# DeltaNet mixer: evacuation steps metered between filler matmuls and pinned on VectorE, decay rows queued behind the inverse, heads split one at a time

## The chip, the cores and the metric

The kernel runs on one core of one Trainium2 chip. The time is the device time of one execution in microseconds, and the number that counts is the median over several runs. The core has a matrix engine (TensorE, PE in the profile), a vector engine (VectorE, DVE), an activation engine (ScalarE, ACT), GpSimd (POOL) and SyncE (SP), which issues nearly all the transfers (DMA). Each engine takes its instructions in a fixed order that is settled when the program is compiled, and waits on semaphores for what other engines make. PSUM holds matmul results in eight banks; SBUF holds everything else.

## What is computed

The reference is a decoder trunk of two layers over 1024 positions of width 1024: layer 0 mixes with a gated DeltaNet, layer 1 with sliding-window attention, and each layer goes on with a convolutional MLP and a per-layer embedding. The change lies in the DeltaNet mixer, and for a small part in the output projection that both mixers share. Cut to what matters:

```python
proj = x @ w_in
qkv = silu(causal_dwconv(proj[..., :3 * hk], conv_w))        # 4 taps along the positions
z = proj[..., 3 * hk:4 * hk]                                 # the gate, 8 heads of 128
q, k = l2norm(q), l2norm(k)
g = -exp(a_log) * softplus(a_in + dt_bias)                   # decay, per head and position
# per head, in chunks:
gcs = cumsum(g); decay = exp(gcs_i - gcs_j) for i >= j
lmat = strictly lower part of (beta * k k^T * decay)
u0, wk = (I + lmat)^-1 [beta * v, beta * exp(gcs) * k]
for each chunk:
    u = u0 - wk s;  o = (q * exp(gcs)) s + (q k^T * decay) u
    s = exp(gcs_last) * s + k_dec^T u
o = rmsnorm(o, norm_w) * silu(z)
out = o @ w_out
```

## The kernel before

Activations are held transposed: 128 channels on the partitions, 1024 positions along the free dimension. A tile of that shape is called a slot tile; 40 slots of SBUF are handed out by a small list (`Slots.get` takes the slot that has been free longest, `put` gives one back). A tile that takes over a slot waits for the last reader of the tile that had it.

*Projections as filler.* Each of the 32 tiles of q, k, v and gate (`act_tile`, `gate_tile`, L452 to L482) is a product of eight 128x128 weight blocks with the normalized input, in three passes each (high and low parts in float32r, `passes`, L215), for two halves of 512 positions: 24 matmuls a half. These products are written as a Python generator, `stream` (L496), that yields after each matmul. The rest of the mixer calls `fill(n)` (L484) wherever TensorE would wait for another engine, and so n filler matmuls are written out there. `until` (L513) fills until a tile that is needed exists. When the projections are used up, the generator goes on with the first part of the output projection (`OutProj.first`, L865), five of the eight heads' share.

*What follows a half tile.* As soon as its 24 matmuls are written, the generator writes the evacuation (L468: PSUM times the norm's row factor, on VectorE, into a padded tile `zp`), the convolution (`conv`, L320: a first tap on ScalarE, three taps as scalar_tensor_tensor on VectorE, L323) and a SiLU on ScalarE (L470). The gate has only an evacuation (L480) and a SiLU.

*Orders.* In the mixer TensorE's instructions are pinned: `E.pinned` (L327) calls `keep_in_program_order`, named `pin`, which puts an instruction behind the one written before it on the same engine. The other engines are pinned in a few places only; elsewhere the compiler's scheduler chooses an order from its own idea of when inputs are ready.

*One head* (loop at L823). `stage1(h)` (L594) loads two rows of decays from DRAM, spread over all partitions (512 KB each, L599 and L606), makes the decay matrix E from the first (L601 on VectorE, L603 and L604 on ScalarE), transposes k, sums its squares on ScalarE (L616), makes kd (L618) and the triangular matrix A (L637), sends A through DRAM to GpSimd, which inverts its 16x16 diagonal blocks in 30 small steps (L652 to L658), and stores them to DRAM (L660, L661). `stage1c(h)` does the same for q and makes the masked products (L682). `stage2(h-1)` (L765) is the recurrence of the head before: eight chunks, each with the chain product, t (L779), product, u (L782 on ScalarE), product, state update st (L792 for the first chunk, L794 after), with 5, 5 and 4 fillers between. `norm_factor` and `stage2b(h-1)` (L810) scale the output of a head (L812), transpose it and multiply it by the gate (L819). `stage1v(h)` turns v. `stage1b(h)` (L708) loads the inverted blocks as R and X (L713, L714) and completes the inverse from blocks of 16 to 128 by products on TensorE (L721 to L761). For head 0, 100 fillers stand ahead of `stage1b`.

*Start.* Four half tiles (k and q of head 0) are begun while the input comes in: they hold all three PSUM banks of the fillers' pool `mm` and one of the three of the pool `d`. Behind them VectorE and ScalarE work out the decays for all heads (L519 to L570), 84 fillers, and then the cumulated decays are written to DRAM (L589).

*Output projection.* `split_first` (L862) splits five heads' outputs at once into high and low parts (`split`, L245: ScalarE copies the high part, VectorE subtracts, L251), 1024 positions wide; then `first(m)` runs eight tiles of 30 matmuls as filler. The attention layer uses the same class, and its stream waits until five outputs exist (L1163).

Of the kernel before, what the change touches and what calls it, by code (L numbers as in the profile page):

```python
# [8 lines left out]
F32 = mybir.dt.float32  # L9
# [7 lines left out]
P = 128  # L17
# [3 lines left out]
NCH = T // P  # L21
# [26 lines left out]
SLOTW = T + 4  # L48
SKEW = 8
NLAST = 4  # L50

# [45 lines left out]
def hs(h):  # L97
    return slice(h * 512, (h + 1) * 512)
# [11 lines left out]
def kernel(  # L110
# [215 lines left out]
    def delta_layer():  # L326
# [123 lines left out]
        outs = []  # L450

        def act_tile(m, name, res, key):  # L452

            begun = m % HA == 0 and m // HA <= 1
            if not begun:
                wh, wl = load_w(a_in[m], D)
            for i in range(2):
# [5 lines left out]
                if i == 0:  # L463
                    z = S.wide("zp")
                    G.memset(z[:, 0:CA - 1], 0.0)
                    y = S.get(name)
                a, b = i * 512, (i + 1) * 512
                V.tensor_tensor(z[:, CA - 1 + a:CA - 1 + b], ps, rb[:, a:b], MUL)  # L468
                conv(y, z, aconv[:, m * CA:(m + 1) * CA], CA, a, b)
                A.activation(y[:, a:b], y[:, a:b], AF.Silu)  # L470
            res[key] = y

        def gate_tile(h, res):
            wh, wl = load_w(a_in[24 + h], D)
            for i in range(2):
                ps = pmt()
                yield from passes(ps, wh, wl, xs, i)
                if i == 0:
                    z = S.get("zs")
                V.tensor_tensor(z[:, hs(i)], ps, rb[:, hs(i)], MUL)  # L480
            A.activation(z[:, :], z[:, :], AF.Silu)
            res[h] = z  # L482

        def fill(n=1 << 30):  # L484

            for _ in range(n):
                if next(main, S) is S:
                    break

        def load_h(t, m):  # L490
            nc.sync.dma_start(t[:, 0:T], xT[m * P:(m + 1) * P, :])

        op = OutProj(a_out, outs, load_h)
        q, k, v, zs, st = {}, {}, {}, {}, {}

        def stream():  # L496
            yield from act_tile(HA, "kT", k, 0)
            yield from act_tile(0, "qT", q, 0)
            yield from act_tile(2 * HA, "vT", v, 0)
            yield from gate_tile(0, zs)  # L500
            for h in range(1, HA):
                yield from act_tile(HA + h, "kT", k, h)
                yield from act_tile(h, "qT", q, h)
                yield from act_tile(2 * HA + h, "vT", v, h)
                yield from gate_tile(h, zs)
            for xh, xl in xs:
# [85 lines left out]
        fill(FG3)  # L592

        def stage1(h, kT):  # L594
            hsl = slice(h * NCH, (h + 1) * NCH)
            junk = sm.tile([P, P], F32, tag="junk", name="junk", bufs=1)
            ssk = sm.tile([P, NCH], F32, tag="ssk", name="ssk")
            rw = S.get("row")
            nc.sync.dma_start(rw[:, :], rowd[0, h:h + 1, :].partition_broadcast(P))  # L599
            ee = S.get("E")  # L600
# [4 lines left out]
            rw = S.get("row")  # L605
            nc.sync.dma_start(rw[:, :], rowd[1, h:h + 1, :].partition_broadcast(P))  # L606

# [100 lines left out]
        def stage1b(h, s):  # L708
# [3 lines left out]
            r = S.get("R")  # L712
            nc.sync.dma_start(r.c3(), mat(xd[par, 1]))  # L713
            nc.sync.dma_start(x.c3(), mat(xd[par, 0]))  # L714
# [50 lines left out]
        def stage2(h, s, FS=FS, FO=FO):  # L765
# [5 lines left out]
            for c in range(NCH):  # L771
# [3 lines left out]
                else:  # L775
                    E.matmul(ch(ps, 0), ch(kT, c), st, start=True, stop=True)
                    fill(FS)
                    t = sm.tile([P, P], F32, tag="t", name="t")
                    V.scalar_tensor_tensor(t, ch(ps, 0), s["nse"][:, c:c + 1], ch(vv, c), MUL, ADD)  # L779
                E.matmul(ch(ps, 1), ch(r, c), t, start=True, stop=True)  # L780
# [8 lines left out]
                if c < NCH - 1:  # L789
                    st2 = sm.tile([P, P], F32, tag="st", name="st")  # L790
                    if c == 0:
                        V.tensor_copy(st2, ch(ps, 2))  # L792
                    else:
                        V.scalar_tensor_tensor(  # L794
                            st2, st, egl[:, h * NCH + c:h * NCH + c + 1], ch(ps, 2), MUL, ADD)
                    st = st2
# [13 lines left out]
        def stage2b(h, s, zs, n=FV):  # L810
            o, kd, f = s["vv"], s["kd"], s["f"]
            pin(V.tensor_tensor(o.c3(), o.c3(), col(f[:, :], NCH, P), MUL))  # L812
            fill(n)
# [33 lines left out]
    class OutProj:  # L847
# [13 lines left out]

        def split_first(self):  # L862
            self.xs = self.parts(0, NP1)

        def first(self, m):  # L865
            t = S.get("h")
            self.load_h(t, m)
            self.h.append(t)
            wh, wl = load_w(self.w[m, :, 0:NP1 * P], NP1 * P)
            for h in range(2):  # L870
                ps = pmt()
                yield from passes(ps, wh, wl, self.xs, h)
                V.tensor_tensor(t[:, hs(h)], t[:, hs(h)], ps, ADD)
            if m == KT - 1:
# [98 lines left out]
    def swa_layer(xs, nrm, hd):  # L973
# [181 lines left out]
        def stream():  # L1155
# [6 lines left out]
            S.put(rb)  # L1162
            while len(outs) < NP1:  # L1163
                yield
            op.split_first()
            for m in range(KT):
# [545 lines left out]
```

## Time and profile before

| | us |
|---|---|
| median of 3 runs | 2745.27 (2741.79 to 2749.13) |
| the profiled execution | 2740.68 |
| its span, first to last instruction | 2738.8 |
| TensorE busy | 2640.8 (96%) |
| VectorE busy | 1792.9 (65%) |
| ScalarE busy | 1114.9 (41%) |
| GpSimd busy | 1191.4 (43%) |
| mean granted TensorE clock | 0.99 |

The profile is that of one execution. A row of instructions names the line of the kernel, the engine, the operation, the tile written and the tiles read (buffer numbers left out), and in brackets how long the engine was idle before it and what ended that idle time. A row of waits reads "engine, tile, line, then what it waited for: us in total, times, longest". A row of a stretch of time gives the busy time of TensorE, its weight loads, VectorE, ScalarE and GpSimd with the counts of instructions, then the granted TensorE clock (1.00 is full speed), the DMA engines' busy share and GB/s. Of a matmul only the start is exact; ends are modelled.

### The profile page before, as it was taken

To read this page: it belongs to the slowest core of one execution; us is meant where nothing else is said; L and a number is where in the kernel's file an instruction comes from. 1 tells how busy PE (TensorE), PEld (TensorE's weight loads), DVE (VectorE), ACT (ScalarE), POOL (GpSimd) and SP (SyncE) were. 2 spreads that over 40 slices of the span, in tenths; PEclk is the share of its full clock that TensorE was granted. 3 is DMA by queue.
4 is the path that set the end of the run, shared out by engine and by line. 5 is a ranking of instruction groups with operands and counts; after the bars stand their busy time and mean duration, and the time that the engine had idled before them with its cause. 6 is when DMAs were issued, how large, how long until landed. Compare 5 with 4: busy or idle time off the path is not lost. (4 is left out here: it accounts for less than half of the span.)

```text
span 2738.8 us, 35465 instructions
## 1 busy us (share of the span) xinstructions
PE 2640.8 (96%) x12914; PEld 2130.2 (78%) x12914; DVE 1792.9 (65%) x2645; ACT 1114.9 (41%) x2176; POOL 1191.4 (43%) x1132
## 2 busy tenths in 40 slices
PE   9899999999999999999999999999999999999998
PEld 7788787878777887888778776667778888888786
DVE  6555555564787777677774437775877767677745
ACT  5443443442643333333353225554533333333443
POOL 4444443442554444444532323335644444444354
PEclk9999999999999999999999999999999999999999
DMA  5222211232325555555432221122255555554323
GB/s 176 89 73 58 67 55 56 67 95 78 109 84 187 181 182 180 203 198 181 161 117 71 90 59 49 46 92 100 81 187 187 182 191 178 199 198 167 103 93 110
DMA packets 167215, 340.85 MB, mean 124 GB/s; under 512 B 38912, under 2 KB 91648, under 8 KB 167040
## 3 DMA queue, kind: packets, MB, share of 16 engines
q1 hardware_dynamic: 166176, 337.20, 37.2%
q8 instruction: 102, 1.67, 0.3%
q10 hardware_dynamic: 864, 1.38, 0.1%
q14 instruction: 73, 0.60, 0.1%
HBM read 232.56 MB, written 99.68 MB: 121 GB/s over the span
## 5 line engine op out<-in xcount | busy, mean ns | idle before, releaser
L202 POOL TENSOR_TENSOR wlo<-wraw,whi 128x512 fp32r<-128x512 f32 (+1 forms) x204 | 269.8, 1340 | 380.6 <-ACT whi L199 344.1
L153 PE MATMUL mm<-xh,whi 128*128 128x512 f32 x856 | 356.2, 416 | 3.9 <-ACT xh L255 2.8
L153 PE MATMUL mm<-xh,wlo 128*128 128x512 f32 x856 | 347.9, 406 | 0.0
L153 PE MATMUL mm<-xl,whi 128*128 128x512 f32 x856 | 346.0, 404 | 0.8 <-DVE xl L256 0.8
L212 POOL TENSOR_TENSOR dlo<-draw,dhi 128x256 fp32r<-128x256 f32 (+1 forms) x160 | 163.1, 1020 | 332.9 <-ACT dhi L211 295.7
L1234 POOL TENSOR_TENSOR wlo<-wraw,whi 128x512 fp32r<-128x512 f32 x132 | 192.6, 1466 | 147.7 <-ACT whi L1233 145.4
L1234 POOL TENSOR_TENSOR wlo<-sa,whi 128x512 fp32r<-128x512 f32 x132 | 194.1, 1470 | 141.0 <-ACT whi L1233 141.0
L153 PE MATMUL d<-gh,dhi 128*128 128x512 f32 x576 | 228.7, 397 | 4.7 <-DVE h L1350 4.2
L153 PE MATMUL d<-gl,dhi 128*128 128x512 f32 x576 | 226.9, 394 | 0.7 <-DVE gl L251 0.7
L153 PE MATMUL d<-gh,dlo 128*128 128x512 f32 x576 | 227.3, 395 | 0.0
L1350 DVE TENSOR_TENSOR h<-h,d 128x512 f32<-128x512 f32 x288 | 193.1, 680 | 32.6 <-PE d L153 32.2
L199 ACT CAST whi<-wraw 128x1024 fp32r<-128x1024 f32 (+3 forms) x122 | 100.1, 822 | 238.5 <-PE mm L153 123.4
L153 PEld LDWEIGHTS mm<-xh,wlo 128*128 128x128 f32 x856 | 163.3, 191 | 33.6 <-POOL wlo L202 0.2
L153 PEld LDWEIGHTS mm<-xh,whi 128*128 128x128 f32 x856 | 163.6, 191 | 30.6 <-ACT xh L255 3.2
L153 PEld LDWEIGHTS mm<-xl,whi 128*128 128x128 f32 x856 | 163.5, 191 | 26.9 <-DVE xl L256 1.4
L153 PE MATMUL mm<-t34h,whi 128*128 128x512 f32 x352 | 139.4, 396 | 3.7 <-DVE zv L1394 3.0
L153 PE MATMUL mm<-t34l,whi 128*128 128x512 f32 x352 | 139.6, 397 | 3.2 <-POOL t34l L919 3.2
L153 PE MATMUL mm<-x1l,whi 128*128 128x512 f32 x352 | 138.9, 395 | 0.2 <-DVE x1l L919 0.2
L153 PE MATMUL mm<-x1h,whi 128*128 128x512 f32 x352 | 138.8, 394 | 0.0
L153 PE MATMUL mm<-t34h,wlo 128*128 128x512 f32 x352 | 138.7, 394 | 0.0
L323 DVE SCALAR_TENSOR_TENSOR yf<-zv,fcv,yf 128x1024 f32<-128x1024 f32 (+1 forms) x92 | 121.5, 1321 | 26.3 <-ACT yf L321 26.2
L153 PE MATMUL mm<-x1h,wlo 128*128 128x512 f32 x352 | 138.2, 392 | 0.0
(382 smaller groups left out, 6564.0 us busy)
## 6 DMA issues: line engine op xcount, KB each, us to landing
hf<-h SPq DMA_DIRECT2D x160, 512.0 KB, 3.3
h<-hf SPq DMA_DIRECT2D x160, 512.0 KB, 4.2
wraw<-f_up SPq DMA_DIRECT2D x88, 512.0 KB, 3.3
draw<-f_down SPq DMA_DIRECT2D x144, 128.0 KB, 2.1
wraw<-a_in SPq DMA_DIRECT2D x32, 512.0 KB, 3.5
wraw<-g_w SPq DMA_DIRECT2D x24, 512.0 KB, 3.3
row<-rowd SPq DMA_DIRECT2D x16, 512.0 KB, 3.7
wraw<-b_in SPq DMA_DIRECT2D x12, 512.0 KB, 3.6
```

Source lines behind the costliest of these rows:

```text
L153: i = nc.tensor.matmul(*a, **k)
L199: A.copy(hi, raw)
L202: G.tensor_tensor(lo[:, i:j], raw[:, i:j], hi[:, i:j].bitcast(F32), SUB)
L212: G.tensor_tensor(lo, raw, hi[:, :].bitcast(F32), SUB)
L323: V.scalar_tensor_tensor(dst[:, a:b], z[:, a + i:b + i], w[:, i:i + 1], dst[:, a:b], MUL, ADD)
L1234: G.tensor_tensor(lo, src, hi.bitcast(F32), SUB)
L1350: V.tensor_tensor(t[:, hs(h)], t[:, hs(h)], ps, ADD)
```

## The change

Three things are edited, all in how and where instructions are written out; no matmul is added or removed.

First, what follows a half tile is no longer written at once. The evacuation and each of the three taps become steps in a list, `later`. `fill` takes one step from the list after every third filler (`EACH = 3`); `until` takes steps before it fills; `flush` empties the list ahead of the output projection. Each step's VectorE instruction is pinned, and so are t, the state updates and the low parts of the first output split.

Second, the loads of the decay rows (`load_row`) are put on SyncE's queue behind the load of R written last (`r_load`), which is that of the head before, and behind each other. The first head's rows have none ahead.

Third, the output projection's first tile (m = 0) splits one head at a time, in halves, and runs that head's six matmuls before it goes to the next head; both PSUM banks are taken together. It waits for each head's output alone, so that the attention layer's own wait for five is gone. Beside it the scaling of a head's output (L812) is done in two halves.

```diff
+EACH = 3
...
+        later = []
         def act_tile(m, name, res, key):
...
+            def evacuate(i, ps):
+                if i == 0:
+                    t.extend((S.wide("zp"), S.get(name)))
+                    G.memset(t[0][:, 0:CA - 1], 0.0)
+                z, y = t
+                a, b = i * 512, (i + 1) * 512
+                pin(V.tensor_tensor(z[:, CA - 1 + a:CA - 1 + b], ps, rb[:, a:b], MUL))
+                A.activation(y[:, a:b], z[:, a:b], AF.Copy, scale=w[:, 0:1])
+
+            def tap(i, j):
+                z, y = t
+                a, b = i * 512, (i + 1) * 512
+                pin(V.scalar_tensor_tensor(y[:, a:b], z[:, a + j:b + j], w[:, j:j + 1], y[:, a:b], MUL, ADD))
+                if j == CA - 1:
+                    A.activation(y[:, a:b], y[:, a:b], AF.Silu)
+                    if i:
+                        res[key] = y
...
-                V.tensor_tensor(z[:, CA - 1 + a:CA - 1 + b], ps, rb[:, a:b], MUL)
-                conv(y, z, aconv[:, m * CA:(m + 1) * CA], CA, a, b)
-                A.activation(y[:, a:b], y[:, a:b], AF.Silu)
+                later.append(lambda i=i, ps=ps: evacuate(i, ps))
+                for j in range(1, CA):
+                    later.append(lambda i=i, j=j: tap(i, j))
...
         def fill(n=1 << 30):
             for _ in range(n):
                 if next(main, S) is S:
                     break
+                steps[0] += 1
+                if steps[0] % EACH == 0 and later:
+                    later.pop(0)()
...
             while h not in d:
-                fill(1)
+                if later:
+                    later.pop(0)()
+                else:
+                    fill(1)
...
+        def load_row(t, i, h):
+            with tc.issue_after(r_load[-1].ins) if r_load else ExitStack():
+                r_load.append(nc.sync.dma_start(t[:, :], rowd[i, h:h + 1, :].partition_broadcast(P)))
...
-            nc.sync.dma_start(r.c3(), mat(xd[par, 1]))
+            r_load.append(nc.sync.dma_start(r.c3(), mat(xd[par, 1])))
...
-                    V.scalar_tensor_tensor(t, ch(ps, 0), s["nse"][:, c:c + 1], ch(vv, c), MUL, ADD)
+                    pin(V.scalar_tensor_tensor(t, ch(ps, 0), s["nse"][:, c:c + 1], ch(vv, c), MUL, ADD))
...
-                        V.scalar_tensor_tensor(
-                            st2, st, egl[:, h * NCH + c:h * NCH + c + 1], ch(ps, 2), MUL, ADD)
+                        pin(V.scalar_tensor_tensor(
+                            st2, st, egl[:, h * NCH + c:h * NCH + c + 1], ch(ps, 2), MUL, ADD))
...
-            pin(V.tensor_tensor(o.c3(), o.c3(), col(f[:, :], NCH, P), MUL))
+            for b in range(2):
+                v = o.c3()[:, 4 * b:4 * b + 4, :]
+                pin(V.tensor_tensor(v, v, col(f[:, 4 * b:4 * b + 4], 4, P), MUL))
...
-        def split_first(self):
-            self.xs = self.parts(0, NP1)
...
+            ps2 = [pmt(), pmt()]
+            if m == 0:
+                self.xs = []
+                for k in range(NP1):
+                    while len(self.outs) <= k:
+                        yield
+                    o = self.outs[k]
+                    hi, lo = S.get("oh", F32R), S.get("ol", F32R)
+                    for h in range(2):
+                        A.copy(hi[:, hs(h)], o[:, hs(h)])
+                        pin(V.tensor_tensor(lo[:, hs(h)], o[:, hs(h)], hi[:, hs(h)].bitcast(F32), SUB))
+                    S.put(o)
+                    self.xs.append((hi, lo))
+                    for h in range(2):
+                        for w, x in ((wh, hi), (wh, lo), (wl, hi)):
+                            E.matmul(ps2[h], ch(w, k), x[:, hs(h)], start=k == 0 and w is wh and x is hi,
+                                     stop=k == NP1 - 1 and w is wl)
+                            yield
...
-            while len(outs) < NP1:
-                yield
-            op.split_first()
```

More of the change, by code (lines that the diff above doesn't have):

```diff
@@ L477, in gate_tile, with flush @@
                 yield from passes(ps, wh, wl, xs, i)
[L478 to L482, printed above, removed]
+                later.append(lambda i=i, ps=ps: evacuate(i, ps))
+        def flush():
+            while later:
+                later.pop(0)()
         def fill(n=1 << 30):
@@ L488, in fill @@
                     break
+                steps[0] += 1
+                if steps[0] % EACH == 0 and later:
+                    later.pop(0)()
+        steps = [0]
         def load_h(t, m):
@@ L494, in delta_layer @@
         q, k, v, zs, st = {}, {}, {}, {}, {}
+        r_load = []
         def stream():
@@ L598, in stage1 @@
             rw = S.get("row")
-            nc.sync.dma_start(rw[:, :], rowd[0, h:h + 1, :].partition_broadcast(P))
+            load_row(rw, 0, h)
             ee = S.get("E")
@@ L605, in stage1 @@
             rw = S.get("row")
-            nc.sync.dma_start(rw[:, :], rowd[1, h:h + 1, :].partition_broadcast(P))
+            load_row(rw, 1, h)
             kd = S.get("kd")
@@ L869, in first @@
             wh, wl = load_w(self.w[m, :, 0:NP1 * P], NP1 * P)
+            ps2 = [pmt(), pmt()]
[16 more added lines that the diff above has]
+                            yield
             for h in range(2):
-                ps = pmt()
-                yield from passes(ps, wh, wl, self.xs, h)
-                V.tensor_tensor(t[:, hs(h)], t[:, hs(h)], ps, ADD)
+                if m:
+                    yield from passes(ps2[h], wh, wl, self.xs, h)
+                V.tensor_tensor(t[:, hs(h)], t[:, hs(h)], ps2[h], ADD)
             if m == KT - 1:
```

21 lines of the change are left out of this document (13 added, 8 removed).

## Prediction

> **What bounds the kernel now.** I read the page first, then the busy time by stage, then who waits for whom on TensorE in the stage that the change touches.
>
> ```profile
> span 2738.8 us, 35465 instructions
> ...
> PE 2640.8 (96%) x12914; PEld 2130.2 (78%) x12914; DVE 1792.9 (65%) x2645; ACT 1114.9 (41%) x2176; POOL 1191.4 (43%) x1132
> ```
> ```profile
> 0.00:740.00 740.00, 698.41 (x4021) 581.30 (x4022) 427.26 (x735) 316.92 (x813) 311.42 (x460) 0.98 0.27 82
> ```
>
> TensorE is the bound. The DeltaNet mixer lies in the first 740 us, and there TensorE is idle for 41.6 us (740 less 698.41). No edit removes a matmul, so the change can be worth only what it does to these idle times and to the clock that falls behind them. The whole prize is near 1.5% of the run. TensorE's waits between 30 and 740 us, longest first:
>
> ```profile
> PE d L153 <- DMA R<-xd: 10.3, 3, 6.0
> PE s L153 <- DVE st L794: 5.8, 5, 1.9
> PE d L157 <- DVE vT L812: 5.1, 4, 2.0
> PE d L157 <- DVE kd L618: 3.1, 1, 3.1
> ...
> PE mm L153 <- DVE ol L251: 1.6, 1, 1.6
> ```
>
> They are few: eight heads with some fifty steps of the recurrence, and TensorE waited only five times on the state update (L794). The present order is not far from good.
>
> **The change part by part.** All sums are against the profiled execution, 2740.68 us (2738.8 of span and 1.9 around it). It lies 4.6 below the median of 2745.27, and I carry the difference over to the median.
>
> *The start.* This is the one cost I hold for near certain. The first four product banks (k and q of head 0) are begun before the recurrence is set up, and three of them are all the banks that the filler matmuls have. So the first filler, v of head 0, waits for the first evacuation.
>
> ```profile
> 46.61 0.61 PE L153 MATMUL mm<-xh,whi 128*128 128x512 f32 x1 [0.17 <-DVE zp L468]
> ```
> ```profile
> 45.89 0.67 DVE L468 TENSOR_TENSOR zp<-mm,rb 128x512 f32<-128x512 f32 x1
> ...
> 51.56 0.19 DVE L556 TENSOR_SCALAR dt<-dt 128x64 f32<-128x64 f32 x1
> ...
> 65.14 0.23 DVE L570 TENSOR_TENSOR dt<-dt,ea 128x64 f32<-128x64 f32 x1
> ```
> ```profile
> 48.10 1.28 ACT L547 ACT_TABLE_LOAD   x1
> ...
> 51.11 0.26 ACT L551 ACTIVATE dt<-dt 128x64 f32<-128x64 f32 x1
> ```
>
> Today that evacuation runs at 45.89, nineteen us ahead of the end of the decay chain (L543 to L570), because VectorE's order is free. After the change it is first written out at the third filler, and it is pinned behind the VectorE instruction written before it, which is L570. TensorE's order is pinned too, so nothing else can fill the hole. When does L570 end if nothing is interleaved? ScalarE's part took from 48.10 to 51.37, so 3.3 us with its two table loads. VectorE's part is 16 instructions, L556 to L570, of 0.19 to 0.23 us, with a reciprocal somewhat longer: 3.7 us. From 48.10 that is 55.1; ScalarE can begin up to 1.3 earlier, since kT's two copies go. With the evacuation's 0.67, TensorE starts between 54.4 and 55.8 instead of 46.61. I take **+8.5** (7.8 to 9.2). It is paid in full, for everything after it is placed by TensorE's progress.
>
> *Decay rows behind the inverse.* The edit queues a head's two row loads on SyncE's queue behind the load of R of the head before. Two of the seven pairs stand ahead of their R today, those of heads 1 and 5; the others are behind it already.
>
> ```profile
> 74.45 0.37 SPq L599 DMA_DIRECT2D row<-rowd  x1
> ```
> ```profile
> 415.71 0.33 SPq L599 DMA_DIRECT2D row<-rowd  x1
> 424.67 0.33 SPq L606 DMA_DIRECT2D row<-rowd  x1
> 425.91 0.37 SPq L713 DMA_DIRECT2D R<-xd  x1
> ```
>
> Head 1's rows are loaded together with head 0's, so its decay matrix sits on ScalarE amid head 0's sums of squares, on which L618 and TensorE wait:
>
> ```profile
> 82.34 1.04 ACT L603 ACTIVATE E<-E 128x1024 f32<-128x1024 f32 x1
> ...
> 87.92 1.28 ACT L604 ACT_TABLE_LOAD   x1
> 89.22 1.06 ACT L604 ACTIVATE E<-E 128x1024 f32<-128x1024 f32 x1
> ```
> ```profile
> 94.31 0.84 PE L157 MATMUL d<-ident,qT 128*128 128x128 f32 x4 [3.06 <-DVE kd L618]
> ```
> ```profile
> 80.00:100.00 20.00, 15.49 (x81) 12.68 (x80) 11.49 (x24) 16.29 (x44) 5.92 (x5) 0.91 0.25 87
> 120.00:140.00 20.00, 16.33 (x99) 13.97 (x98) 9.52 (x10) 3.87 (x7) 5.52 (x10) 1.00 0.41 112
> ```
>
> That is 3.4 us of ScalarE, more than the wait of 3.06, so the wait goes, and with it the lower clock of that stretch: 0.09 of 20 us, 1.8. What is late next is head 0's R, which already costs the 3.67 us missing in 120 to 140. Its chain (A, inverse on GpSimd, two DMAs) runs from A at its own pace, so it takes back about 1.3. Net **-3.6** (0 to -4.9).
>
> R's long wait, 6.0, is not a matter of rows. R of head 4 takes, by the code's list of free slots, the slot of head 3's gate, freed just before, and its load leaves SyncE when L819 has read that slot:
>
> ```profile
> 423.35 1.22 DVE L601 TENSOR_TENSOR E<-row,gcc 128x1024 f32<-128x1024 f32 x1
> 424.49 1.40 DVE L819 SCALAR_TENSOR_TENSOR kd<-d,anorm,zs 128x512 f32<-128x512 f32 x2
> ```
>
> L819 ends at 425.89 and the load goes at 425.91. Counting the slots for the new order gives R the same one. Only L601 moves away from in front of L819: **-1.0** (0 to -1.2). I expect some 5 us of that wait to stay.
>
> *The output scaled in halves (L812).* The transposes wait for the first half alone.
>
> ```profile
> L812 DVE TENSOR_TENSOR vT<-vT,f 128x1024 f32<-128x1024 f32 x8 | 10.8, 1349 | 1.8 <-POOL f L808 1.8
> ```
>
> Half of 1.35, less a second instruction's fixed part, is 0.6, at four waits: **-2.4** (0 to -5.1, if the better order also removes the rest).
>
> *Splitting singly.* The first split falls from whole to half tiles, but VectorE's part is now pinned in the recurrence of head 6: 1.6 falls by half, and some clock comes back: **-1.5** (-3.4 to +1). In the second layer the same waits are
>
> ```profile
> PE mm L153 <- DVE ol L251: 3.6, 2, 3.3
> ```
>
> and I take **-1.5** (-3.6 to +1).
>
> *One step for three fillers, in written order.* A half tile's four steps (evacuation, three taps) run today as soon as they can, so up to four stand in front of t (L779) or the state update. With one step for three fillers, and nine fillers from state update to t, it is at most three.
>
> ```profile
> L779 DVE SCALAR_TENSOR_TENSOR t<-s,nse,vT 128x128 f32<-128x128 f32 x56 | 19.5, 348 | 19.0 <-PE s L153 18.7
> ```
> ```profile
> L323 DVE SCALAR_TENSOR_TENSOR qT<-zp,const,qT 128x512 f32<-128x512 f32 x48 | 44.2, 920 | 9.4 <-ACT qT L321 8.9
> ```
> ```profile
> 1437.38 5.58 PE mm L153 x24
> ```
>
> A filler takes 0.23 us (5.58 by 24). The recurrence of a head has 107 fillers; over seven heads, at 24 a half tile, three quarters of them with taps, that is 23 groups of four steps. Today the state update costs 5.8 us, 0.25 a group. Spacing takes some of it away, and pinning puts new waits in, since a first tap waits for ScalarE's copy (8.9 us in 16 groups, 0.56 each) and t now stands behind it. No row shows the pinned order; the ends are -5.8 and +14 (below), and the nearest row is today's own 5.8. I take a third off: **-2.0**.
>
> Sum: 8.5 - 3.6 - 1.0 - 2.4 - 1.5 - 1.5 - 2.0 = **-3.5**, so 2737.2 for the profiled execution and 2741.8, in round numbers **2742**, for the median. Everything after the mixers keeps its instructions.
>
> Two rules of the Trainium skill bear on this. The clock: behind R's wait it was granted at 0.83 over 20 us.
>
> ```profile
> 420.00:440.00 20.00, 13.95 (x76) 12.07 (x75) 10.90 (x15) 6.39 (x7) 4.45 (x3) 0.83 0.20 58
> ```
>
> The Trainium skill ("TensorE: Matmul & The Clock Gate", "Why this matters for your kernels") warns of idle gaps over about 3 us, each of which brings half clock. By that rule the new hole at the start costs another 1.8 (0.09 of 20 us, as in 80 to 100), and the sum would be -1.7. The trace agrees only in part: 3.67 us of idle in 120 to 140 left the clock at 1.00.
>
> The taps: most take 0.75 us, some far longer.
>
> ```profile
> L323 DVE SCALAR_TENSOR_TENSOR kT<-zp,const,kT x48: 735/752/2779, 47.5 to 552.7; 128x512 f32<-128x512 f32 x48
> ```
>
> The Trainium skill ("SBUF — State Buffer", "Who interferes with whom") says that a VectorE instruction with two SBUF inputs contends with GpSimd's reads, so that one blocks the other. A tap has two such inputs. That speaks against pinning taps in front of t, and it adds to the second rival.
>
> **The rivals.** *Faster, as the pinned order does all it can:* start 7.8, first rows -4.9, R -1.2, scaling -4.0, state updates -5.8, the two splits -3.4 and -3.0. That is -14.5: 2731. For it speaks that today's waits come where bursts of taps stand before L794; against it that five waits in fifty steps leave little to order.
>
> *Slower, as the pinned waits move onto t.* If a group begins between the state update and t, VectorE must do evacuation 0.67, wait 0.56, tap 0.75 and t 0.35: 2.3 us. TensorE has five fillers and a small product, about 1.4, to cover it. That is 0.9 lost, and with a tap of 2.8 us some 3. At a mean of 0.6 over 23 groups it is +14 instead of -2, so +12.3: 2758. It decides from about 0.42 a group, where the sum passes +8.2. For it speaks that rigid order; against it that TensorE never waited for t (L779) so far.
>
> *The row edit does nothing:* if head 1's rows did not hold L618, its -3.6 falls away, and with the rest the time is 2745, still no change.
>
> **How the numbers follow.** A measurement of this kernel tells about 0.3% (8.2 us) from no change. Forecast, with the row rival in it: 0.42, between 2737 and 2753. Faster rival 0.38, since nearly every wait that it removes stands in today's trace. Slower rival 0.20, since its waits do not stand there yet. The cases of both signs hold most of the chance beside a likeliest one of 2742. The range reaches to 2724 (the faster case with the other 4.8 us of R's long wait and some clock behind it gone as well) and to 2759 (the slower case).
>
> **What would show it.** Right: a TensorE gap of 8 us near 47, released by zp, with L570 just before it; no gap at 94; R of head 4 still late by about 5 us; waits for L812 shorter by 0.6; rows of heads 1 and 5 behind R. Wrong: no gap at the start, or t (L779) among TensorE's releasers with more than 5 us in total, or the R wait gone.

## The result, and the profile after

| | before | after |
|---|---|---|
| median of 4 runs, us | 2745.12 | 2783.80 (2782.80 to 2785.61) |
| ratio to before, 95% interval | | 1.0135 (1.0123 to 1.0147) |
| the profiled execution, us | 2740.68 | 2784.41 |

The change makes the kernel 1.35% slower. I forecast 2742 and a range to 2759; the time lies outside it. The head of the page of the changed kernel:

```profile
span 2782.7 us, 35467 instructions
...
PE 2648.9 (95%) x12914; PEld 2133.1 (77%) x12914; DVE 1805.3 (65%) x2663; ACT 1116.6 (40%) x2186; POOL 1195.5 (43%) x1132
```

The span grew by 43.9 and TensorE's busy time by only 8.1 with the same 12914 matmuls: it waits more. Where, is read best by laying matmul n of one trace beside matmul n of the other; both have the same number. The second column says by how much the changed kernel is later ("offset") when the kernel before stands at the first.

| time in the kernel before, us | offset of after, us | what lies between |
|---|---|---|
| 71 | +9.2 | the start |
| 122 | +3.1 | head 0's kd and A |
| 140 | +6.3 | the wait for head 0's R |
| 783 | +27.5 | the recurrences of heads 0 to 7 |
| 1779 | +33.2 | layer 0's MLP, the second layer's projections |
| 1880 | +43.3 | the second layer's split |
| 2723 | +43.8 | the rest |

The new line numbers: t is L822 (was L779), state update L835 and L837 (L792, L794), scaling L857 (L812), gate product L864 (L819), kd L661 (L618), evacuation L470 (L468), taps L476 (L323), low parts L923 (L251). TensorE's waits between 30 and 780 us in the changed kernel (us in total, times, longest), against the list of before in the prediction:

```profile
PE s L154 <- DVE t L822: 23.8, 19, 3.3
PE d L154 <- DMA R<-xd: 10.9, 3, 5.5
PE mm L154 <- DVE zp L470: 8.7, 1, 8.7
...
PE d L158 <- DVE vT L857: 2.5, 3, 1.0
PE s L154 <- DVE st L837: 1.9, 2, 1.6
...
PE s L154 <- DVE st L835: 1.3, 1, 1.3
```

The first row is new: t had no row before. The third is the start's gap, which was forecast. Scaling (5.1 before) and state updates (5.8 and 1.1 before) got shorter together, as meant. So 23.8 were added at t to take about 6 away elsewhere.

The start's gap, with the end of the decay chain (L608) and the first evacuation in front of it:

```profile
53.98 0.22 DVE L608 TENSOR_TENSOR dt<-dt,ea 128x64 f32<-128x64 f32 x1
54.13 0.68 DVE L470 TENSOR_TENSOR zp<-mm,rb 128x512 f32<-128x512 f32 x1
```
```profile
54.86 0.79 PE L154 MATMUL mm<-xh,whi 128*128 128x512 f32 x1 [8.73 <-DVE zp L470]
```

One wait for t in full, in head 0's recurrence. VectorE's rows:

```profile
170.49 0.29 DVE L835 COPY st<-s 128x128 f32<-128x128 f32 x1 [1.22 <-PE s L154]
170.70 4.59 DVE L476 SCALAR_TENSOR_TENSOR kT<-zp,const,kT 128x512 f32<-128x512 f32 x3
175.22 0.34 DVE L822 SCALAR_TENSOR_TENSOR t<-s,nse,vT 128x128 f32<-128x128 f32 x1
```

GpSimd's and TensorE's beside them:

```profile
171.35 3.39 POOL L203 TENSOR_TENSOR wlo<-wraw,whi 128x512 fp32r<-128x512 f32 x2
```
```profile
172.31 0.40 PE L154 MATMUL mm<-xl,whi 128*128 128x512 f32 x1
175.61 0.73 PE L154 MATMUL s<-t,R 128*128 128x128 f32 x2 [2.90 <-DVE t L822]
...
176.56 0.63 PE L154 MATMUL mm<-xh,whi 128*128 128x512 f32 x1
176.99 0.63 PE L154 MATMUL mm<-xl,whi 128*128 128x512 f32 x1
```

Three taps written between the state update and t stand in front of t, because all are pinned. They take 4.59 us, 1.53 each, and GpSimd splits weights (L203) during most of it. TensorE has its nine fillers and the chain product, and then nothing. Afterwards its fillers start 0.43 apart instead of 0.23, at half clock. From 160 to 180 us the offset rises from 6.1 to 10.0: this burst costs 2.90 of waiting and about one more behind it.

In the second layer's split, the VectorE and TensorE rows:

```profile
1828.10 1.22 DVE L1099 TENSOR_TENSOR q<-q,qa 64x1024 fp32r<-64x1024 f32 x1 [1.37 <-ACT qa L1097]
1829.35 1.22 DVE L1100 TENSOR_TENSOR q<-q,qb 64x1024 fp32r<-64x1024 f32 x1
1830.60 1.29 DVE L923 TENSOR_TENSOR ol<-oT,oh 128x512 fp32r<-128x512 f32 x2
```
```profile
1831.35 0.80 PE L154 MATMUL mm<-ol,whi 128*128 128x512 f32 x1 [5.23 <-DVE ol L923]
```

The low part is pinned behind the VectorE instruction that happens to be written before it. Here that is the last conversion of q (L1100), which comes behind L1099, and L1099 waits for ScalarE. TensorE's waits on the low parts there went from 3.6 to 10.0 in total: this one is 5.23, and another of 3.52 (at 1840.31) ends behind an unrelated copy (L1185).

### The profile page after: what moved, and what is told of

Same layout as the page of the kernel before. It is cut to its first block, busy times and chain, and to the rows that moved or that the text cites. A ratio compares the mean times of both kernels' runs of the same rounds, so it can differ in the third digit from the quotient of the medians.

```text
span 2782.7 us, 35467 instructions
## 1 busy us (share of the span) xinstructions
PE 2648.9 (95%) x12914; PEld 2133.1 (77%) x12914; DVE 1805.3 (65%) x2663; ACT 1116.6 (40%) x2186; POOL 1195.5 (43%) x1132
## 4 chain that ended last, share of the span: by engine, by line
PE 60%; DVE 8%; issue 2%; ACT 2%; POOL 2%; DMA 0%; DVEq 0%; POOLq 0%; ACTq 0%
PE mm L154 35%; PE d L154 22%; PE s L154 2%; DVE sc L1158 1%; POOL wlo L1292 1%; DVE yf L324 1%; DVE sc L1134 1%; PE d L158 1%; ACT sc L1151 1%; DVE sa L1311 0%; DVE yf L1366 0%; DVE h L1408 0%; DVE sq L1030 0%; DVE h L952 0%; POOL wlo L203 0%
## 5 line engine op out<-in xcount | busy, mean ns | idle before, releaser
L203 POOL TENSOR_TENSOR wlo<-wraw,whi 128x512 fp32r<-128x512 f32 (+1 forms) x204 | 268.8, 1334 | 403.8 <-ACT whi L200 372.9
L154 PE MATMUL d<-gh,dhi 128*128 128x512 f32 x576 | 229.5, 398 | 10.2 <-DVE h L1408 9.7
L324 DVE SCALAR_TENSOR_TENSOR yf<-zg,fcv,yf 128x1024 f32<-128x1024 f32 (+1 forms) x92 | 132.1, 1436 | 18.2 <-ACT yf L322 16.6
L154 PEld LDWEIGHTS d<-gh,dhi 128*128 128x128 f32 x576 | 108.2, 188 | 42.5 <-DVE h L1408 14.8
```

The lines of the kernel that those rows point to most:

```text
L154: i = nc.tensor.matmul(*a, **k)
L203: G.tensor_tensor(lo[:, i:j], raw[:, i:j], hi[:, i:j].bitcast(F32), SUB)
L324: V.scalar_tensor_tensor(dst[:, a:b], z[:, a + i:b + i], w[:, i:i + 1], dst[:, a:b], MUL, ADD)
```

## The experiments

The theory after seeing the trace: the new order of VectorE costs the time, at three places (the start, t, the second layer's split). The rival: the rhythm itself, steps written late, or another part of the change. Each kernel is the changed one or the one before with a few lines edited. Ratios are to the kernel before, run on the same chip in the same session; its own median moved from 2745 to 2749 between sessions, so ratios are to be compared and not medians. Where the intervals overlap I go by the offsets, but each kernel was traced once. Up to the first split the changed kernel and e3 have the same code, and their offsets agree to 0.9 us; at 71 us e4 and f4 have the same code and differ by 1.5. A difference of a microsecond or two therefore says little.

| kernel | median, us | ratio (95%) | offset at 122 | at 783 | at 1779 | at 1880 |
|---|---|---|---|---|---|---|
| changed | 2783.8 | 1.0135 (1.0123 to 1.0147) | +3.1 | +27.5 | +33.2 | +43.3 |
| e1: start free | 2781.5 | 1.0133 (1.0105 to 1.0161) | +1.5 | +24.5 | +27.5 | +37.7 |
| e2: steps, t, updates free | 2748.9 | 1.0007 (0.9993 to 1.0020) | -3.7 | -7.1 | -1.9 | +8.3 |
| e3: low parts free | 2773.4 | 1.0100 (1.0073 to 1.0127) | +3.4 | +34.1 | +41.2 | +41.3 |
| e4: before with rows only | 2743.7 | 0.9988 (0.9972 to 1.0004) | -3.3 | -3.6 | -2.0 | +0.2 |
| f1: t and updates free | 2761.5 | 1.0057 (1.0037 to 1.0076) | +3.3 | +3.3 | +6.3 | +16.5 |
| f2: pinned, none before t | 2741.0 | 0.9981 (0.9968 to 0.9995) | +3.3 | -10.8 | -12.4 | -1.3 |
| f3: no new pins | 2742.4 | 0.9980 (0.9966 to 0.9994) | -3.6 | -7.1 | -1.4 | -1.3 |
| f4: before with rows, halves | 2743.9 | 0.9996 (0.9982 to 1.0010) | -4.9 | -6.4 | -3.6 | -2.5 |
| g1: no new pins, slots later | 2736.7 | 0.9952 (0.9934 to 0.9970) | -4.9 | -9.2 | -9.5 | -9.9 |
| g2: f2, low parts and start free | 2734.1 | 0.9938 (0.9915 to 0.9961) | +1.2 | -10.8 | -5.3 | -5.3 |
| g3: none before t, no new pins | 2729.2 | 0.9931 (0.9909 to 0.9953) | -5.0 | -17.1 | -13.1 | -13.1 |
| g4: f2, low parts free | 2739.5 | 0.9967 (0.9955 to 0.9978) | +3.6 | -8.9 | -3.7 | -2.1 |

**e1, the start.**

```diff
-                pin(V.tensor_tensor(z[:, CA - 1 + a:CA - 1 + b], ps, rb[:, a:b], MUL))
+                e = V.tensor_tensor(z[:, CA - 1 + a:CA - 1 + b], ps, rb[:, a:b], MUL)
+                if not begun:
+                    pin(e)
...
+                if begun:
+                    flush()
```

> The changed kernel, but the four half tiles begun ahead (k and q of head 0) are evacuated and convolved as soon as they are written, unpinned, as in the kernel before. If the 8.7 us wait near 47 us comes from the pin behind the decay chain (L570), it goes and the time falls from 2783.8 to about 2775 (2773 to 2777), with the rest of the offset against the kernel before unchanged. Rival: the offset at the start is given back later anyway, for R of head 0 sets the pace there; then the time falls by less than 3 us.

The gap near 47 went, but only 3 us of it are left at 783 (+24.5 against +27.5), and the time cannot be told from that of the changed kernel. That is the rival's number, but not for its reason: TensorE does not wait longer for R of head 0, it waits 5.05 for kd, where the changed kernel waits 0.2. ScalarE's and TensorE's rows:

```profile
83.98 1.06 ACT L652 ACTIVATE E<-E 128x1024 f32<-128x1024 f32 x1 [3.82 <-DVE E L650]
...
86.35 1.06 ACT L653 ACTIVATE E<-E 128x1024 f32<-128x1024 f32 x1
...
89.26 0.26 ACT L665 ACTIVATE junk<-d 128x128 f32<-128x128 f32 x1
```
```profile
92.39 2.08 PE L154 MATMUL d<-kT 128*128 128x128 f32 x8 [5.05 <-DVE kd L667]
```

Head 0's sums of squares (L665) stand behind its decay matrix E on ScalarE, and E is late because the loads of its rows are. SyncE's rows in e1, and then in the changed kernel:

```profile
76.56 0.33 SPq L197 DMA_DIRECT2D wraw<-a_in  x1
77.01 0.84 SPq L641 DMA_DIRECT2D row<-rowd  x2
```
```profile
82.55 0.94 SPq L635 DMA_DIRECT2D row<-rowd  x2
85.62 12.46 SPq L197 DMA_DIRECT2D wraw<-a_in  x2
```

In e1 a load of weights goes ahead of the rows, in the changed kernel it goes behind them. So TensorE is 9 us earlier in e1, but VectorE can begin E only 3.5 earlier (82.72 against 86.26). e1's edit therefore moved something on SyncE too, and it does not show by itself what the start's gap is worth. f4 and g3 have no gap, their rows leave first (at 73.06 and 72.94), and at 122 us they are 8.0 and 8.1 ahead of the changed kernel (-4.9 and -5.0 against +3.1); they lack its other pins too.

**e2 and f1, the pins.** e2 takes the pins off steps, t and updates; f1 off t and updates alone.

```diff
-                    pin(V.scalar_tensor_tensor(t, ch(ps, 0), s["nse"][:, c:c + 1], ch(vv, c), MUL, ADD))
+                    V.scalar_tensor_tensor(t, ch(ps, 0), s["nse"][:, c:c + 1], ch(vv, c), MUL, ADD)
...
-                        pin(V.scalar_tensor_tensor(
-                            st2, st, egl[:, h * NCH + c:h * NCH + c + 1], ch(ps, 2), MUL, ADD))
+                        V.scalar_tensor_tensor(
+                            st2, st, egl[:, h * NCH + c:h * NCH + c + 1], ch(ps, 2), MUL, ADD)
```

> The changed kernel with the steps, t and the state updates not pinned; the list and its rhythm (one step for three fillers) stay, and so do the rows, the halves and the single split with its pinned low parts. If the pins cost the time (first evacuation behind the decay chain 8.7, t behind taps some 24 with the half clock after it), it falls to about 2750 (2745 to 2756) and t is no longer among TensorE's releasers with more than 5 us. Rival: it is the metering, steps written late, so that banks and tiles come late; then only the start comes back and the time stays near 2775.

> The changed kernel with t and the state updates not pinned, while the evacuations and taps keep their pins. If it is t standing behind the steps that costs the recurrence its 24 us, the matmul after the mixer (near 735 us) comes some 20 us earlier than in the changed kernel and the time is about 2761 (2757 to 2767). The start and the second layer's split stay as they are. Rival: the steps' own written order holds other work too (a chain of taps that waits for ScalarE stands in front of everything that is pinned later); then less than half of it comes back, 2770 or more.

Both came out as the theory had it. TensorE's waits in f1:

```profile
PE mm L154 <- DVE zp L470: 8.7, 1, 8.7
PE s L154 <- DVE st L837: 6.2, 4, 2.1
PE s L154 <- DVE t L822: 3.4, 4, 1.3
```

With t and the updates free, t's 23.8 fall to 3.4 and the mixer ends 24.2 earlier (27.5 less 3.3), while the start's gap stays. In e2 the waits on t are 0.4 and the mixer ends 7.1 before that of the kernel before, with the rhythm of one step for three fillers unchanged. So the rhythm alone costs nothing. The low parts keep their pins in both, and both still lose 10.2 between 1779 and 1880, as e1 does.

**e3, the low parts.**

```diff
-                        pin(V.tensor_tensor(lo[:, hs(h)], o[:, hs(h)], hi[:, hs(h)].bitcast(F32), SUB))
+                        V.tensor_tensor(lo[:, hs(h)], o[:, hs(h)], hi[:, hs(h)].bitcast(F32), SUB)
```

> The changed kernel with only the pin on the low parts of the first output split removed. If that pin costs the attention layer its 10 us (the low part stands behind the last conversion of q), the time falls to about 2773 (2771 to 2777), and the waits for ol at the second layer's split go to under 4 us. Rival: the waits come from splitting one head at a time, six matmuls against one head's copy and subtraction; then the time stays within 3 us of 2783.8.

The second layer's split gives back its 10 us: the offset is 41.2 before it and 41.3 behind it, where the changed kernel goes from 33.2 to 43.3, and the waits on ol are 2.4. But in the mixer of the traced execution the same edit costs 6.6 (34.1 against 27.5), which I had not expected; 4.7 of it are there by 620 us. Three of the free low parts now stand in front of a first state update (L835), and TensorE's waits on it go from 1.3 to 4.9:

```profile
635.72 5.45 DVE L923 TENSOR_TENSOR ol<-kd,oh 128x512 fp32r<-128x512 f32 x3
641.09 0.28 DVE L835 COPY st<-s 128x128 f32<-128x128 f32 x1
```

That execution took 2781.9, which is 8.5 above the median, so what the others lost in the mixer is not known.

**e4 and f4, rows and halves by themselves**, both on the kernel before (rows by `load_row` as in the change, halves by the two-part scaling).

> The kernel before with only the decay rows queued behind the inverse. My term for it was -3.6; the changed kernel's trace shows the matmuls between 60 and 118 us gaining 5.8. So 2739 to 2742 against 2745.1. Rival: the gain is taken back at head 0's R, whose wait grew from 3.8 to 4.6, or at later heads whose E is late; then 2744 to 2747.

> The kernel before with the decay rows behind the inverse and the output's scaling in halves, nothing else. My terms are -3.6 and -2.4; the rows alone gave -3.9 at the end of the mixer. Halves: TensorE's waits on L812 fall from 5.1 to 2.5. So the mixer ends 6 to 7 us earlier than in the kernel before and the time is 2739 (2736 to 2742). If it equals the kernel with all pins removed, the rhythm of one step for three fillers is worth nothing without the pins; if that kernel ends its mixer over 2 us earlier, the rhythm or the single split has a worth of its own.

Rows: 3.6 at 783, and 4.8 counted from 71 us, where this trace already stood 1.2 late. Rows and halves: 6.4. Of the 2.8 between the two, 1.5 stand at 71 us already (+1.2 against -0.3), before any line in which they differ, so 1.3 are left for the halves; the waits on scaling are 3.5, against 5.1 in e4. Neither gain is in the medians, and f4 missed its 2736 to 2742: later stretches, unedited, take it back (see f3).

**f2, g4, g2 and g3, where the steps are written.** In f2 all pins stay, and no step is written among the nine fillers between an update and the next t:

```diff
-        def fill(n=1 << 30):
+        def fill(n=1 << 30, hold=False):
...
+                if hold:
+                    continue
                 steps[0] += 1
...
                     E.matmul(ch(ps, 0), ch(kT, c), st, start=True, stop=True)
-                    fill(FS)
+                    fill(FS, True)
...
-                fill(FO)
+                fill(FO, c < NCH - 1)
```

> The changed kernel with all its pins, but no step is written among the fillers between a state update and the next t (four after the update, five before t); the steps come with the other fillers. If t is late only because steps stand between the update and it, TensorE's waits on t fall from 23.8 us to under 4 and the time to about 2761 (2757 to 2768). Rival: the steps that now gather between t and the state update make the update late in its place; then TensorE's waits on st rise by 10 us or more and the time stays above 2770.

Better than either theory said. f2's waits, and its VectorE rows at the place shown above (t is L824 here, the updates L837 and L839):

```profile
PE mm L154 <- DVE zp L470: 8.7, 1, 8.7
PE d L154 <- DMA R<-xd: 4.3, 1, 4.3
PE s L154 <- DVE st L839: 3.4, 4, 1.6
...
PE s L154 <- DVE t L824: 1.7, 4, 0.6
```
```profile
170.44 0.29 DVE L837 COPY st<-s 128x128 f32<-128x128 f32 x1 [1.21 <-PE s L154]
171.52 0.35 DVE L824 SCALAR_TENSOR_TENSOR t<-s,nse,vT 128x128 f32<-128x128 f32 x1 [0.79 <-PE s L154]
171.79 3.03 DVE L476 SCALAR_TENSOR_TENSOR kT<-zp,const,kT 128x512 f32<-128x512 f32 x2
174.79 0.35 DVE L839 SCALAR_TENSOR_TENSOR st<-st,egl,s 128x128 f32<-128x128 f32 x1
```

The taps are as long as before (3.03 for two), but they lie behind t. Between t and the next update VectorE has a product, ScalarE's u and five fillers to hide them, and TensorE's waits on st stay at 3.4. So the late t needs both: the pin, and steps written in front of it. The part that I had not foreseen is that the wait for head 4's R is gone as well (one wait on R instead of three): its load leaves at 420.76, ahead of the gate product at 426.46, so the changed order of requests gave R another slot (g1 below). Between 400 and 440 us f2 gains 11.7 on the kernel before, the changed kernel 2.5.

> The changed kernel with its pins on steps, t and updates, no step written between an update and the next t, and only the low parts unpinned; the first evacuation still stands behind the decay chain. By the 11 us of the second layer: 2741 - 11 = 2730. Against the same with a free start it shows what the start's 8.7 us wait is worth: 8.7 if it is paid in full, about 3 if the sums of squares of head 0 take the rest back.

> The changed kernel with its pins on steps, t and updates, no step written between an update and the next t (2741.0 with that alone), and besides the low parts unpinned and the first four half tiles evacuated at once. The low parts cost the second layer 11 us in that kernel's trace, the start 8.7 or, by the run with a free start, some 3 net. So 2741 - 11 - 3 = 2727 (2720 to 2731). Rival: the low parts unpinned move in front of a state update in the mixer, as they did in the run that freed them alone (some 6 us): 2733 or more.

> As the kernel with free start and free low parts and no step written between an update and the next t, but with every new pin removed. If the place where the steps are written is what counts and the pins only enforce it, it is 2 to 8 us slower than the pinned one (2729 to 2735), since the scheduler then puts taps in front of updates again (waits on st of 4 us or more). Rival: the pins themselves never help; then it is as fast or faster, 2727 or less.

g4 missed its 2730 by 9.5. The free low parts did end the loss in the second layer (11.1 in f2 from 1779 to 1880, 1.6 in g4, none in g2). But the mixer lost 1.9 (a wait of 3.1 on a first update, as in e3), and the unedited stretch from 783 to 1779 went from -1.6 in f2 to +5.2. g4 and g2 differ by the start: 71 us into the kernel by 8.6 in the traces (+9.6 and +1.0), at 783 by 1.9 (-8.9 and -10.8). What is lost between is e1's wait again, for in g2 too the rows of head 0 leave behind a load of weights (77.93 behind 77.48). g2 missed its 2727: that kd wait came (kd is L669 here, the update L843), and a wait on an update stayed, as its rival said:

```profile
PE d L154 <- DVE kd L669: 5.0, 1, 5.0
PE s L154 <- DVE st L843: 4.4, 2, 3.1
```

g3, without any new pin, was expected to be slower than g2, and its mixer ends 6.3 earlier (-17.1 against -10.8). That its median lies in the range that I gave is luck, for the range was counted from g2's 2727. Yet the trace does not say that the pins hurt in the recurrence. All of the lead is there at 122 us (-5.0 against +1.2, the kd wait and the rows again), and from there to 783 both gain the same, 12.1 and 12.0. So with no step before t the pins on steps, t and updates make no difference in these traces.

What not writing steps before t is worth without pins is read from g3 against f3 (below), which lacks only that. g3's longest waits:

```profile
PE s L154 <- DVE st L839: 5.5, 5, 1.6
PE s L154 <- DVE st L837: 4.1, 2, 3.1
PE d L154 <- DMA R<-xd: 4.0, 1, 4.0
```

In both there is no wait on t, and the waits on updates are no shorter in g3 (9.6 against 8.7 in f3). Of the 8.6 that g3 gains on f3 from 122 to 783, 8.2 lie between 400 and 440 us: the load of head 4's R left before the gate product, as in f2, and f3 waits 5.10 for it.

```profile
413.63 0.38 SPq L758 DMA_DIRECT2D R<-xd  x1
...
419.16 1.41 DVE L866 SCALAR_TENSOR_TENSOR kd<-d,anorm,zs 128x512 f32<-128x512 f32 x2 [0.73 <-PE d L158]
```

So g3's gain over f3 is nearly all the slot of R, and not the place of the steps. g3 is the fastest kernel of the study, 0.7% below the kernel before; between it and g2 or g1 the intervals do not decide.

**g1, the slot of R.** The kernel without new pins, and the slots of a head's output and gate offered after those given back at the same moment:

```diff
-            S.put(o, zs)
+            S.free.extend(((S.n + 0.5, o.i), (S.n + 0.5, zs.i)))
```

> The changed kernel with all new pins removed (its mixer ended 5.7 us before that of the kernel before), and one edit more: a head's output slot and gate slot, when given back, stand behind the slots given back at the same moment, so that R of the next head does not take the gate's slot. If R of head 4 is late because its slot is still read by L864, its 5.1 us wait and the half clock behind it go: 2735 to 2738 after 2742.4, and only head 0's R wait of 4.6 stays. Rival: the load then waits for something else (its blocks in DRAM, X's slot), the wait stays and the time within 2 us of 2742.4.

The wait went as expected. The gate product L864 and SyncE's issue of R for head 4, first in f3 (the same kernel without this edit), then in g1:

```profile
420.12 1.41 DVE L864 SCALAR_TENSOR_TENSOR kd<-d,anorm,zs 128x512 f32<-128x512 f32 x2 [0.73 <-PE d L158]
...
421.55 0.38 SPq L756 DMA_DIRECT2D R<-xd  x1
...
425.61 3.75 PE L154 MATMUL d<-R,A 128*128 128x128 f32 x16 [5.10 <-DMA R<-xd]
```
```profile
415.62 0.38 SPq L756 DMA_DIRECT2D R<-xd  x1
...
424.09 1.41 DVE L864 SCALAR_TENSOR_TENSOR kd<-d,anorm,zs 128x512 f32<-128x512 f32 x2 [0.70 <-PE d L158]
```

In f3 the load leaves 0.02 after L864 has ended, in g1 8.5 before it begins, and TensorE's wait is gone. The stretch behind it, 420 to 440 us, f3 and then g1:

```profile
420.00:440.00 20.00, 14.90 (x92) 13.61 (x91) 9.91 (x14) 8.15 (x9) 2.82 (x4) 0.83 0.31 105
```
```profile
420.00:440.00 20.00, 20.00 (x134) 17.06 (x132) 14.13 (x22) 9.20 (x12) 4.99 (x5) 1.00 0.17 62
```

TensorE is busy throughout and at full clock, and between 400 and 440 us g1 gains 6.3 more than f3. At 783 only 2.1 of it are left, for two waits in the mixer are longer than in f3: one of 2.3 for a gate product (kd, L864) near 350 us, and one on a first update (4.3 for 3.1). That the median fell by 5.7, into the range that I gave, is therefore in part luck: in the traces the lead on f3 grows from 2.1 at 783 to 8.1 at 1779, in the stretch that no edit touches.

**f3, all new pins off.**

> The changed kernel with none of its new pins (steps, t, state updates, low parts); rhythm, rows, halves and the single split stay. If the pins alone made it slower, the mixer ends about 7 us before that of the kernel before (it did so with the steps free) and the second layer's split costs nothing: 2739 (2735 to 2743), 0.3% faster than the kernel before. Rival: splitting singly keeps a cost in the second layer without pins, 2743 to 2747.

The mixer ended 7.1 early as said and the second layer's split cost nothing (from -1.4 to -1.3 over it), yet the median is 2742.4: 5.7 went between 783 and 1779. That stretch holds the MLP, which no kernel here edits. There the offset moved by +5.7 in the changed kernel, +1.6 in e4, +2.8 in f4, -1.6 in f2, +7.1 in e3. It may depend on when the MLP begins beside the transfers and GpSimd's work. It may as well be scatter between executions: nearly all executions of the kernel before lie between 2737.8 and 2756.7, without any edit. No run here tells the two apart. In the mixer f3 ends 0.7 before f4, and 2.0 counted from 71 us, so without pins the rhythm and the single split are worth little.

## Why the prediction was wrong

**The step that failed: the pinned order.** I priced "one step for three fillers, in written order" at -2.0, a third off today's state-update waits. That row was the wrong neighbour: it prices the waits that the order removes, and not the new ones. Freeing t and the updates is worth 24.2, and with t's pin kept but no step in front of it (f2) the wait goes as well. The mechanism stood among the rivals ("the pinned waits move onto t"), with the right place and a chance of 0.20, but mis-sized at 0.6 us a group, +14. The trace has 23.8 in 23 groups, 1.03 each, before the clock. Two sizes were short. I let one group's evacuation, wait and a single tap stand before t, where the rhythm of three gives up to three steps in the nine fillers, as in the rows at 170 us; I had counted these three myself, a few lines earlier. And I took a long tap for an exception, though the taps of q had a mean of 0.92 beside a median of 0.75 in the kernel before. My argument against the rival, that TensorE had never waited for t, was no evidence: until then the scheduler had been free to put t first.

The Trainium skill ("SBUF — State Buffer", "Who interferes with whom") says that a VectorE instruction with two SBUF inputs contends with GpSimd's reads. The trace agrees: three taps took 1.53 each beside L203. I cited the rule and did not carry it into the rival's mean of 0.6.

**The second layer's split** was -1.5 with a bound of +1; it cost 10.1 (33.2 to 43.3). I looked for what is pinned in the recurrence and did not ask which instruction is written ahead of the low parts in the other layer that uses the class. It is a conversion behind another that waits for ScalarE (5.23 of the 10.0 us of waits). With the low parts free the loss there is 0.1 in e3 and f3, and 10.1 to 11.1 in every kernel that keeps their pin.

**The start** had the gap right (8.73 for 8.5), released by zp, right behind the end of the decay chain. "Paid in full" is not refuted. The free start brought only 3 us at the mixer's end in e1 and 1.9 in g2 (against g4), but in both head 0's rows leave behind a load of weights, and TensorE waits 5 us for kd instead. Where the rows go first in both kernels, g4 against g3, 8.6 stand at 122 us and 8.2 at 783; the two differ in the other pins too, which cost g2 nothing against g3 between 122 and 783. What does fail is the reason that I gave, that everything after is placed by TensorE's progress: head 0's E is placed by the loads of its rows.

**Rows.** They carry two terms, -3.6 and -1.0 at head 4's R, so 4.6; e4 has 3.6 at 783 and 4.8 from 71 us on. The parts came out less well than the sum: from 71 to 122 us it gained 4.5 (I had 4.9 before R's answer), of which head 0's R took back 2.5 by 140 where I had allowed 1.3. Head 4's R fell from 6.0 to 5.1. **Halves** -2.4: 1.3 to 2.8 by f4 against e4, and the waits on scaling went from 5.1 to 3.5 there and to 2.5 in the changed kernel. **Head 4's R**: some 5 us were to stay, and 5.5 stayed; g1 shows the slot as its cause. **The first layer's split**: no isolated run; its waits are short in the changed kernel, where the offset falls by 3.4 between 600 and 620 us (by 1.6 in f4, which has the old split). Its pin helped there, for in e3, g4 and g2 the free low parts overtake a first state update.

**The clock.** I said that the Trainium skill's warning of idle gaps over about 3 us ("TensorE: Matmul & The Clock Gate", "Why this matters for your kernels") holds only in part. The traces bear this out in both directions. In the changed kernel a gap of 2.90 was followed by half clock, and the clock of 160 to 180 us fell to 0.91; in the kernel before, 1.98 us of idle in all gave 0.91 over 400 to 420 us, while 3.67 left 1.00 over 120 to 140. For the hole at the start I had worked out 1.8 by that rule. The offset of 9.2 is 0.5 above the gap of 8.73; the kernel before had a lower clock there as well (0.91 over 40 to 60 us).

The sum by what was measured: 9.2 at the start, less 6.1 by 122 us; +24.4 from there to 783; +5.7 in unedited work; +10.1 at the second split; 0.5 in the rest. That is 43.8, against 38.7 between the medians, since the profiled execution of before was 4.4 below its median and that of the changed kernel 0.6 above. The same matmuls from 122 to 783, in the kernel before and in the changed one:

```profile
122.00:783.00 661.00, 628.71 (x3682) 523.30 (x3681) 384.13 (x651) 270.54 (x735) 275.92 (x395) 0.98 0.24 73
125.10:810.50 685.40, 633.14 (x3682) 523.44 (x3682) 383.99 (x665) 276.96 (x744) 275.07 (x398) 0.99 0.24 72
```

TensorE's idle time grew by 20.0 (from 32.3 to 52.3): 23.8 at t, 6.3 less at updates and scaling, 0.6 more at R, and 1.9 in short waits. The other 4.4 are busy time. They are not more half clock, for the granted clock is no lower than before; what they are stays open.

## What to carry to other kernels

A pin does not only fix an order that one likes; it puts each instruction behind whatever is written before it, so for each pin one has to name that instruction and what it waits for, in every place where the code is used. On the engine that feeds a short recurrence, pinned filler work belongs behind the step that the matrix engine waits for next (between t and the update here). Without pins t was not waited for (f3 and g3), and the place where the steps were written hardly changed the waits of the recurrence. The best kernel has the change's rows, halves, single split and list, none of its pins, and no step between update and t, but its lead over the kernel that lacks only the last of these (f3) comes nearly all from another slot for head 4's R. So an edit on one engine can move loads and slots elsewhere (e1, f2, g3), and a time is put down to the edit only when the other orders have been compared too.

## What the runs showed of the hardware

A tap took 0.74 us where GpSimd was all but idle (at 166.38 in the changed kernel), and three in a row 1.53 each, most of it beside GpSimd's split of weights; such a burst held VectorE, which takes its instructions in order, for 4.59. A wait of 2.90 us on TensorE was followed by half clock: fillers started 0.43 us apart instead of 0.23 behind it. Neither 2.90 nor 3 is a bound, for 1.98 us of idle in 20 lowered the clock to 0.91 in one stretch and 3.67 left it at 1.00 in another. The stretch with the unedited MLP moved by -1.6 to +7.1 us between kernels traced once each, which is as large as most of the terms that were predicted.
